# Taking a fourth token block's expert activations from gathered rows, while its value products stay dense

## The chip, the cores and the metric

The kernel runs on one core of a Trainium2 chip. The metric is device time in microseconds, the median of three runs. Each run executes the whole layer once. The profile is one further execution.

## What is computed

The reference is one layer of a streaming encoder over 1024 tokens of width 1024: a mixing part (attention over latents, "MLA", and gated linear attention, "GLA") and then an expert part, which is what the change touches. Cut to that:

```python
q = (h @ w_q).reshape(B, L, 8, 2, 128)                 # 8 heads, two halves
s = einsum('blhpd,pnd->blhpn', q, sub_keys)            # scores against 2 x 128 keys
top_s, top_i = top_k(s, 16)
...                                                    # 16 best of the 16 x 16 sums
idx  = ...                                             # expert numbers, of 128 * 128 = 16384
gate = softmax(best_s)
act  = gelu(einsum('bpd,bphkd->bphk', h, u_tab[idx]))  # one row of u for each pick
coef = act * gate
out  = einsum('bphk,bphkd->bpd', coef, v_tab[idx])     # one row of v for each pick
```

Every token picks 8 x 16 = 128 of 16384 experts. Each expert has a row of 1024 numbers in `u` and one in `v`.

## The kernel before

**Two ways through the experts.** The 1024 tokens are eight blocks of 128. Blocks 0 to 2 take the picked rows by indirect DMA ("gathers"): for each of the 128 picks one DMA brings one row of `u` for every token of the block (a tile of 128 x 1024 numbers, 512 KB) and another brings the rows of `v`. VectorE makes a dot product of each `u` tile with the tokens (L1303), ScalarE the GELU of 16 of them at a time (L1305), and VectorE adds each `v` tile, scaled, to an accumulator (L1312). That is 3 x 128 x 2 = 768 gathers. Blocks 3 to 7 (640 tokens, `ND`) go through all experts on TensorE: for each of 128 keys `e`, a u stage multiplies the tokens with 128 rows of `u` and takes the GELU; a coefficient step multiplies the result by a matrix of gates that is zero where an expert was not picked (L1433); and v stages multiply the coefficients with `v` and add up. Each product is three matmuls of a high and a low half (L80 to L82), and the low half of each 512 KB weight tile is made by VectorE (L74) once ScalarE has made the high half (L73).

**Sizes.** A u stage has 640 tokens, more than one PSUM tile holds, so it runs twice over 320 columns (`HD`): 2 x 8 x 3 = 48 matmuls for a key. A v stage works on a group `q` of four keys and one half of the output columns: 4 keys x 5 blocks x 3 = 60 matmuls of 512 columns, five PSUM tiles added to the accumulator in SBUF at L1450. A group has two such halves.

**Order of the work.** Tokens go in two groups of four blocks. After MLA, GLA and routing of group 0 follow MLA(1), mix(1) (GLA and output projection), route(1), then "build" (`gate_matrix` writes the gates of the dense blocks to HBM, d_gate), then the dense stage. The u stages of keys 0 to 21 stand in route(1), those of 22 to 53 in build (both write their activations to HBM, d_act), and those of 54 to 127 between the v stages. So the v stages of the first twelve groups have no u stage beside them, and from the end of group 11 on four u stages go with each group, the last two behind group 29.

**Pace of the gathers.** The gathers are a generator, `self.G`. `bg` steps it by `rate` gathers for each weight tile that is asked for (`weights`), and in MLA for each step of `merge`. A gather is issued by GpSimd after ScalarE's last cast (`pace`), and its VectorE work is placed behind the last low half made (`lag`). The row tiles are a ring of `NROW`; the dot or add of a row is placed NROW - 2 gathers after its issue. The rates are `R_MLA` in MLA(1) (until its last unit), `R_MIX`, `R_ROUTE`, `R_BUILD` and `R_DENSE`. By the code the calls that step the generator are 144 in MLA(1), 50 weight tiles in mix(1), 38 in route(1), 32 in the u stages of build (of which 27 by the rate of build), and 202 in the dense stage.

**Queues.** Weight tiles, gates (1280 KB for a group, 512 bytes at a stretch) and activations come by SyncE's queue, in order; gathers, and MLA's stored keys and values, by GpSimd's. A weight tile has two raw buffers (`wr`) and two pairs of halves (`wh`, `wl`).

Of the kernel before, what the change touches and what calls it, by code (L numbers as in the profile page):

```python
# [20 lines left out]
P = 128  # L21
# [11 lines left out]
NK = 128  # L33
LEVELS = (64, 32, 16, 8, 4, 2, 1)
NGB = 3
NROW = 6
DB = list(range(GB, NB)) + list(range(NGB, GB))
ND = len(DB) * P
HD = ND // 2
EG = 4  # L40
NLEAD = 54
PACE, LAG = True, True
# [9 lines left out]
BANKS = [dict(zip(("S", "tr", "mm", "pv"), map(int, str(x)))) for x in (BA, BB)]  # L52
NGA, NGR, F_MLA = 14, 14, 0.9
RA0, NRU, NLATE = 7, 22, 5
R_MLA, R_MIX, R_ROUTE, R_BUILD, R_DENSE = 0.0, 1.5, 0.6, 2.6, 3.0


class Layer:
# [85 lines left out]
    def build(self, debug=None):  # L144
# [4 lines left out]
        self.rate = 0.0  # L149
        self.owed = self.nwl = self.wlp = 0.0  # L150
        self.pref = {}
        self.raws = {}
        self.picks = {}
        with ExitStack() as ctx:
# [24 lines left out]
            self.d_gab = dt("d_gab", [2, 2 * NC, P, GT])  # L179
            self.d_h = dt("d_h", [T, D])  # L180
            self.d_n2 = dt("d_n2", [T, D])
            self.d_act = dt("d_act", [NLEAD, P, ND])
            self.d_n2t = dt("d_n2t", [2, P, NC, ND - GT]) if ND > GT else None
            self.d_gate = dt("d_gate", [P, ND // 32, NK * 32])
            self.small = self.pool(ctx, "small", 3)
            self.sm = self.small
            with ExitStack() as c0:
# [10 lines left out]
                with ExitStack() as c:  # L198
# [6 lines left out]
                    keys = self.gate_keys()[NGF:NGR]  # L205
                    self.route(0, {hp: keys[hp - RA0:hp - RA0 + 1] if hp < 15 else keys[max(15 - RA0, 0):] for hp in range(RA0, 16)}, self.lead_gate)
                    self.tokens_last()
            self.G = self.gather_all(list(range(NGB)))
            self.rate = R_MLA
            with ExitStack() as c:  # L210
                self.mh = self.pool(c, "mh", 2)
# [958 lines left out]
    def norm_ffn(self, g):  # L1170
        nc, a = self.nc, self.a
        t0 = g * GT
        hb = self.hb
        nh, nl = self.n2 = [self.t(self.arp, [P, NC, ND if g else GT], F32R, "ar", 2) for _ in range(2)]
        if g and ND > GT:
            for i, x in enumerate(self.n2):
                nc.gpsimd.dma_start(x[:, :, GT:], self.d_n2t[i].bitcast(F32R))
        gain = self.t(self.wp, [P, D], F32, "wr")
        self.bcast_row(gain, a["norm_ffn"], D)
        for b in range(GB):  # L1180
            rows = slice(t0 + b * P, t0 + (b + 1) * P)
            nc.sync.dma_start(self.d_h[rows], hb[:, b])
            n = self.row_norm(self.wk, self.sm, hb[:, b], gain)
            if g * GB + b < NGB or self.debug:
                nc.sync.dma_start(self.d_n2[rows], n)
        if g == 0 and NGF:
            self.lead_gate(self.gate_keys()[0], ("w_q", 0))
        for b in range(GB):
            self.transpose_split(self.psum, hb[:, b], nh[:, :, b * P:(b + 1) * P], nl[:, :, b * P:(b + 1) * P])
            yield  # L1190
# [15 lines left out]
    def route(self, g, fill, step):  # L1206

        nc, a = self.nc, self.a
        nh, nl = self.n2
        pk = []  # L1210
        pool = self.gp if g == 0 else self.pb
        for b in range(GB):
            d = dict(gate=self.t(pool, [P, 8, 16], F32, "gate", GB))
            if g * GB + b < NGB:
                d["idi"] = self.t(self.wk, [P, 8, 16], I32, "idi", NGB)
            else:
                d["ij"] = self.t(pool, [P, 2, 8, 16], F32, "ij", GB if g else GB - NGB)
            pk.append(d)
            self.picks[g * GB + b] = d
        rt = self.t(self.g1, [P, 4096], F32, "yl")  # L1220
        self.r_oh = [rt[:, 512 * i:512 * i + 512].rearrange("p (w i j) -> p w i j", w=2, j=16) for i in range(3)]
        self.r_sc = rt[:, 1536:2560].rearrange("p (n k) -> p n k", k=NK), rt[:, 2560:3008].rearrange("p (n k) -> p n k", k=112)
        rs = self.t(self.g1, [P, 4096], F32, "yh")
        w5 = lambda x, n: x.rearrange("p (a b c d) -> p a b c d", a=n, b=GB, c=2)
        self.r_cand = rs[:, 0:448].rearrange("p (b k) -> p b k", b=GB)
        self.r_tv = w5(rs[:, 448:576], 1)[:, 0]
        self.r_tf = w5(rs[:, 576:832], 2)
        self.r_ab = w5(rs[:, 832:1088], 2).bitcast(U32)
# [12 lines left out]
        for h in range(8):  # L1241
            s = self.t(self.wk, [P, GB, 2, NK], F32, "gt", 2)
            for p in range(2):
                hp = 2 * h + p
                extra = fill.get(hp, [])
                after = ("w_q", hp + 1) if hp < 15 else None
                nxt = (extra + [after])[0]
                pq, _, _ = self.colproj(("w_q", hp), nh, nl, GT, nxt, 2 if hp < QP else 1)
                qs = r_qs[p]
                nc.scalar.copy(qs, pq)  # L1250
                if p == 1:
                    keyscores(s, 0)
# [12 lines left out]

    def tokens_last(self):

        nc = self.nc
        if ND > GT:
            for i, x in enumerate(self.n2):  # L1270
                nc.sync.dma_start(self.d_n2t[i], x[:, :, NGB * P:].bitcast(F32))
        for b in range(NGB):
            pk = self.picks[b]
            ids = self.t(self.gp, [P, 8, 16], I32, "ids", NGB)
            nc.vector.tensor_copy(ids, pk["idi"])
            pk["idi"] = ids

    def gather_all(self, blks):

        nc = self.nc
        units = [(b, h) for b in blks for h in range(8)]
        queue, held = [], {}
        lag = lambda i: self.after(i, self.dve_last) if LAG else None

# [4 lines left out]
        def start(b):  # L1291
            n2 = self.t(self.gp, [P, D], F32, "n2b", 1)
            nc.sync.dma_start(n2, self.d_n2[b * P:(b + 1) * P])
            acc = self.t(self.gp, [P, D], F32, "acc", 1)
            nc.sync.dma_start(acc, self.d_h[b * P:(b + 1) * P])
            held[b] = n2, acc

        def dot(b, c, u):
# [4 lines left out]
            lag(nc.vector.tensor_tensor_reduce(out=u, in0=u, in1=held[b][0], op0=ALU.mult, op1=ALU.add, scale=1.0, scalar=0.0, accum_out=act[:, 0, k:k + 1]))  # L1303
            if k == 15:
                nc.scalar.activation(act[:, 1], act[:, 0], AF.Gelu)  # L1305

        def add(b, c, v):
            h, k = c // 16, c % 16
# [77 lines left out]
    def u_stage(self, e, nxt, at, behind=None):  # L1386

        n2h, n2l = self.n2
        wh, wl = self.weights(("uT", e), nxt)
        for k in range(2):  # L1390
            ts = slice(k * HD, (k + 1) * HD)
            ps = self.t(self.psum, [P, 512], F32, "tr")
            for c in range(NC):
                s = slice(c * P, (c + 1) * P)
                first = self.mm3(ps[:, :HD], wh[:, s], wl[:, s], n2h[:, c, ts], n2l[:, c, ts], c == 0, c == NC - 1)
                if c == 0 and behind is not None:
                    self.after(first, behind)
            self.nc.scalar.activation(at[:, ts], ps[:, :HD], AF.Gelu)  # L1398

    def lead_gate(self, key, nxt):  # L1400
        self.run(self.raw_gate(1, self.gate_keys().index(key), nxt, "tr", 2))
# [1 line left out]
    def lead_u(self, key, nxt):  # L1403
        e = key[1]
        if e % 6 == 0:
            self.leads = self.t(self.g1, [P, 6, ND], F32, "nl" if e % 12 else "nh", 1)
        at = self.leads[:, e % 6]
        self.u_stage(e, nxt, at)
        self.nc.sync.dma_start(self.d_act[e], at)
# [1 line left out]
    def dense(self, ctx):  # L1411
# [12 lines left out]
        def load_act(e):  # L1424
            if e < NLEAD:
                acts[e] = self.t(self.wk, [P, ND], F32, "at", NAT)
                nc.sync.dma_start(acts[e], self.d_act[e])

        def coef(q, j):
            cf = coefs[q, j] = self.t(self.wk, [P, 2, ND], F32R, "cf", NCF)  # L1430
            at = acts.pop(q * EG + j)
            at3 = at.rearrange("p (b t) -> p b t", t=32)
            (nc.gpsimd if j < CFP else nc.vector).tensor_tensor(at3, at3, gbuf[:, q % 2, :, j], ALU.mult)  # L1433
            self.split(cf[:, 0], cf[:, 1], at)

        def v_stage(q, half):
# [30 lines left out]
        def lead():  # L1467
            for x in seq[:nlead]:
                at = self.t(self.wk, [P, ND], F32, "at", NAT)
                self.u_stage(x[1], order.get(("uT", x[1])), at, self.gm_last if x[1] >= NLEAD - NLATE else None)  # L1470
                nc.sync.dma_start(self.d_act[x[1]], at)
                done[0] += 1
                yield

# [40 lines left out]
    def gate_matrix(self):  # L1515
# [3 lines left out]
        nc = self.nc  # L1519
        G8 = 8  # L1520
        iota = self.iota[:, None, :].broadcast_to([P, G8, NK])
        for d, blk in sorted(enumerate(DB), key=lambda x: x[1]):
            pk = self.picks[blk]
            stage = self.t(self.wk, [P, NK, 32], F32, "big")
            pt = self.t(self.psum, [P, 4, P], F32, "tr")
            for i in range(2):
# [97 lines left out]
```

## Time and profile before

| | us |
|---|---|
| median of three runs | 3879.04 (3875.96 to 3888.12) |
| the profiled execution, its own time | 3874.64 |
| its span, first to last instruction | 3872.9 |
| TensorE busy | 3616.7 (93%) |
| VectorE busy | 3015.7 (78%) |
| ScalarE busy | 1293.6 (33%) |
| GpSimd busy | 1572.3 (41%) |

Engines are PE (TensorE), PEld (its weight loads), DVE (VectorE), ACT (ScalarE), POOL (GpSimd) and SP (SyncE). Records of consecutive instructions of an engine overlap, so the pace of an engine is the distance from one start to the next, and a PE that is shown busy is not at its peak for that.

### The profile page before, as it was taken

The numbers are of one execution on the slowest core, as the hardware profiler recorded it, in microseconds if no ns is written. First come the engines' busy times: TensorE is split into PE (matmuls) and PEld (weight loads), VectorE is DVE, ScalarE is ACT, GpSimd is POOL, SyncE is SP. The second block draws the span as 40 slices with busy tenths as digits, with TensorE's granted clock in tenths as the row PEclk, the third lists the DMA queues.
The fourth block names the chain that finished last, engine by engine and source line by source line (L and its number), as shares of the span: only waits on it lengthen the run. The fifth ranks groups of instructions, "written<-read, shape, count | busy, mean of one in ns | idle before, by whom it ended". The sixth has DMA issues, their size and how long they took to land.

```text
span 3872.9 us, 55720 instructions
## 1 busy us (share of the span) xinstructions
PE 3616.7 (93%) x20279; PEld 3170.8 (82%) x20279; DVE 3015.7 (78%) x6477; ACT 1293.6 (33%) x2711; POOL 1572.3 (41%) x1151
## 2 busy tenths in 40 slices
PE   8899998998799899999999978999999999999999
PEld 8787797777588788788899967767888888898897
DVE  5544444389877577679999997998998888888786
ACT  4655333232366333232243432222222222222221
POOL 2432333335532232322232223444555555656562
PEclk9898998999899998999999989999999999999999
DMA  4433423442323763654467779999998988998895
GB/s 161 142 108 130 131 69 103 135 142 90 126 71 97 235 221 127 253 171 149 131 249 291 277 277 372 357 342 337 319 340 320 325 306 310 327 324 310 293 317 189
DMA packets 356628, 868.92 MB, mean 224 GB/s; under 512 B 30768, under 2 KB 150064, under 8 KB 353536
## 3 DMA queue, kind: packets, MB, share of 16 engines
q1 hardware_dynamic: 216832, 432.49, 32.1%
q0 software_dynamic: 139520, 432.87, 32.1%
q8 instruction: 159, 2.61, 0.3%
q14 instruction: 117, 0.96, 0.1%
HBM read 754.90 MB, written 110.35 MB: 223 GB/s over the span
## 4 chain that ended last, share of the span: by engine, by line
PE 41%; DVE 16%; DMA 9%; issue 3%; ACT 1%; POOL 1%; SPq 0%; DVEq 0%; ACTq 0%; POOLq 0%
PE mm L81 7%; PE mm L80 7%; PE mm L82 7%; DMA wr<-in_vb 5%; PE tr L80 5%; PE tr L82 5%; PE tr L81 5%; DVE wl L74 2%; DVE cf L1540 2%; DVE acc L1312 2%; DVE row L1303 2%; PE mm L1546 2%; DVE cf L1541 1%; DVE big L1450 1%; DMA row<-in_u,ids 1%
## 5 line engine op out<-in xcount | busy, mean ns | idle before, releaser
L73 ACT CAST wh<-wr 128x1024 fp32r<-128x1024 f32 x416 | 436.0, 1049 | 1208.0 <-PE mm L82 400.4
L100 POOL DMA_INDIRECT row<-in_v,ids x384 | 535.7, 1395 | 699.1 <-ACT wh L73 325.1
L100 POOL DMA_INDIRECT row<-in_u,ids x384 | 521.0, 1357 | 665.4 <-ACT wh L73 338.2
L80 PE MATMUL tr<-ar,wh 128*128 128x320 f32 x2048 | 638.7, 312 | 7.3 <-ACT at L1398 5.3
L82 PE MATMUL tr<-ar,wl 128*128 128x320 f32 x2048 | 633.5, 312 | 7.6 <-DVE wl L74 7.5
L81 PE MATMUL tr<-ar,wh 128*128 128x320 f32 x2048 | 636.3, 311 | 0.0
L74 DVE TENSOR_TENSOR wl<-wr,wh 128x1024 fp32r<-128x1024 f32 x322 | 395.0, 1227 | 227.3 <-ACT wh L73 220.7
L81 PE MATMUL mm<-wl,cf 128*128 128x512 f32 x1280 | 514.8, 402 | 11.4 <-DVE wl L74 11.4
L82 PE MATMUL mm<-wh,cf 128*128 128x512 f32 x1280 | 508.3, 397 | 0.0
L1312 DVE SCALAR_TENSOR_TENSOR acc<-row,act,acc 128x1024 f32<-128x1024 f32 x384 | 491.2, 1279 | 4.1 <-DMA row<-in_v,ids 3.5
L80 PE MATMUL mm<-wh,cf 128*128 128x512 f32 x1280 | 451.3, 403 | 35.4 <-ACT wh L73 28.7
L1303 DVE CUSTOM_DVE_ANT_0 row<-row,n2b 128x1024 f32<-128x1024 f32 x384 | 469.2, 1226 | 16.1 <-DMA row<-in_u,ids 16.0
L80 PEld LDWEIGHTS tr<-ar,wh 128*128 128x128 f32 x2048 | 388.7, 190 | 11.9 <-ACT at L1398 5.5
L82 PEld LDWEIGHTS tr<-ar,wl 128*128 128x128 f32 x2048 | 387.0, 190 | 10.3 <-DVE wl L74 10.1
L81 PEld LDWEIGHTS tr<-ar,wh 128*128 128x128 f32 x2048 | 388.4, 190 | 3.5
L74 POOL TENSOR_TENSOR wl<-wr,wh 128x1024 fp32r<-128x1024 f32 x94 | 230.3, 2453 | 333.8 <-ACT wh L73 323.9
L80 PEld LDWEIGHTS mm<-wh,cf 128*128 128x128 f32 x1280 | 241.3, 190 | 105.5 <-ACT wh L73 34.1
L81 PEld LDWEIGHTS mm<-wl,cf 128*128 128x128 f32 x1280 | 243.1, 190 | 76.0 <-DVE wl L74 20.2
L82 PEld LDWEIGHTS mm<-wh,cf 128*128 128x128 f32 x1280 | 243.2, 190 | 55.9
L1450 DVE TENSOR_TENSOR big<-mm,big 128x512 f32<-128x512 f32 x320 | 204.5, 679 | 20.6 <-PE mm L82 20.3
L1546 PE MATMUL mm<-cf,cf 128*128 128x128 f32 x1280 | 162.6, 284 | 27.8 <-DVE cf L1541 27.1
L1546 PEld LDWEIGHTS mm<-cf,cf 128*128 128x128 f32 x1280 | 157.2, 199 | 30.2 <-issue 22.4
(430 smaller groups left out, 7500.4 us busy)
## 6 DMA issues: line engine op xcount, KB each, us to landing
wr<-in_uT SPq DMA_DIRECT2D x128, 512.0 KB
wr<-in_vb SPq DMA_DIRECT2D x128, 512.0 KB
d_gate<-big SPq DMA_DIRECT2D x20, 2048.0 KB
big<-d_gate SPq DMA_DIRECT2D x32, 1280.0 KB
at<-d_act SPq DMA_DIRECT2D x54, 320.0 KB
wr<-in_w_q SPq DMA_DIRECT2D x32, 512.0 KB
d_act<-at SPq DMA_DIRECT2D x32, 320.0 KB
wr<-in_w_ga SPq DMA_DIRECT2D x16, 512.0 KB
```

The lines of the kernel that those rows point to most:

```text
L73: self.pace = self.nc.scalar.copy(hi, src)
L74: i = (eng or self.nc.vector).tensor_tensor(lo, src, hi.bitcast(F32), ALU.subtract)
L80: first = mm(ps, lh, rh, start=start, stop=False)
L81: mm(ps, lh, rl, start=False, stop=False)
L82: self.pe_last = mm(ps, ll, rh, start=False, stop=stop)
L100: i = self.nc.gpsimd.indirect_dma_start(out=out, out_offset=None, in_=self.a[table], in_offset=bass.IndirectOffsetOnAxis(ap=idx, axis=0))
L1303: lag(nc.vector.tensor_tensor_reduce(out=u, in0=u, in1=held[b][0], op0=ALU.mult, op1=ALU.add, scale=1.0, scalar=0.0, accum_out=act[:, 0, k ...
L1312: lag(nc.vector.scalar_tensor_tensor(acc, v, act[:, 1, k:k + 1], acc, ALU.mult, ALU.add))
L1450: nc.vector.tensor_tensor(o, ps[b], o, ALU.add)
L1540: nc.vector.tensor_scalar(gh[:, k], self.iota, tt[:, 1, t + k:t + k + 1], tt[:, 2, t + k:t + k + 1], ALU.is_equal, ALU.mult)
L1541: nc.vector.tensor_tensor(oh, iota, tb(0), ALU.is_equal)
L1546: self.gm_last = nc.tensor.matmul(ps[:, k], oh[:, kk], gh[:, kk], start=True, stop=True)
```

## The change

Blocks 0 to 2 stay as they are, and so do the v stages of blocks 3 to 7. Block 3 gets its 128 x 128 activations from gathered rows of `u`, as blocks 0 to 2 do; they are multiplied into its gates, and the products go through `gate_matrix` in place of the gates, so that its part of the coefficient needs no further product: ScalarE copies it (128 columns) and VectorE's product shrinks to 512 columns. The u stage is left with blocks 4 to 7, 512 tokens, in one pass of 24 matmuls. Block 3's gathers (128 of `u`, none of `v`) stand first in the order; `gate_matrix` takes block 3 last and would first step the gathers as far as its coefficients need. The stored transposes of block 3 (d_n2t) fall away, its normed rows are kept in d_n2, stored activations shrink from 320 to 256 KB for a key, the ring of rows has seven tiles, and three rates rise.

```diff
-NROW = 6
+NROW = 7
 DB = list(range(GB, NB)) + list(range(NGB, GB))
 ND = len(DB) * P
-HD = ND // 2
+NU = GB * P
...
-R_MLA, R_MIX, R_ROUTE, R_BUILD, R_DENSE = 0.0, 1.5, 0.6, 2.6, 3.0
+R_MLA, R_MIX, R_ROUTE, R_BUILD, R_DENSE = 0.3, 2.6, 0.6, 3.0, 3.0
...
-            self.G = self.gather_all(list(range(NGB)))
+            self.G = self.gather_all(list(range(NGB, GB)), list(range(NGB)))
...
-        nh, nl = self.n2 = [self.t(self.arp, [P, NC, ND if g else GT], F32R, "ar", 2) for _ in range(2)]
-        if g and ND > GT:
-            for i, x in enumerate(self.n2):
-                nc.gpsimd.dma_start(x[:, :, GT:], self.d_n2t[i].bitcast(F32R))
+        nh, nl = self.n2 = [self.t(self.arp, [P, NC, GT], F32R, "ar", 2) for _ in range(2)]
...
-            if g * GB + b < NGB or self.debug:
+            if g * GB + b < GB or self.debug:
                 nc.sync.dma_start(self.d_n2[rows], n)
...
-    def gather_all(self, blks):
+    def gather_all(self, half, blks):
...
-        units = [(b, h) for b in blks for h in range(8)]
+        units = [(b, h) for b in half + blks for h in range(8)]
...
-            acc = self.t(self.gp, [P, D], F32, "acc", 1)
-            nc.sync.dma_start(acc, self.d_h[b * P:(b + 1) * P])
+            acc = None
+            if b in blks:
+                acc = self.t(self.gp, [P, D], F32, "acc", 1)
+                nc.sync.dma_start(acc, self.d_h[b * P:(b + 1) * P])
...
                 nc.scalar.activation(act[:, 1], act[:, 0], AF.Gelu)
+                if b in half:
+                    gate = self.picks[b]["gate"][:, h]
+                    nc.vector.tensor_tensor(gate, act[:, 1], gate, ALU.mult)
+                    if h == 7:
+                        self.coefs_of.add(b)
...
+                    if what is add and b in half:
+                        continue
...
-        for k in range(2):
-            ts = slice(k * HD, (k + 1) * HD)
-            ps = self.t(self.psum, [P, 512], F32, "tr")
-            for c in range(NC):
-                s = slice(c * P, (c + 1) * P)
-                first = self.mm3(ps[:, :HD], wh[:, s], wl[:, s], n2h[:, c, ts], n2l[:, c, ts], c == 0, c == NC - 1)
...
-            self.nc.scalar.activation(at[:, ts], ps[:, :HD], AF.Gelu)
+        ps = self.t(self.psum, [P, 512], F32, "tr")
+        for c in range(NC):
+            s = slice(c * P, (c + 1) * P)
+            first = self.mm3(ps, wh[:, s], wl[:, s], n2h[:, c], n2l[:, c], c == 0, c == NC - 1)
...
+        self.nc.scalar.activation(at[:, 0:NU], ps, AF.Gelu)
...
-            (nc.gpsimd if j < CFP else nc.vector).tensor_tensor(at3, at3, gbuf[:, q % 2, :, j], ALU.mult)
+            m = NU // 32
+            nc.scalar.copy(at3[:, m:], gbuf[:, q % 2, m:, j])
+            nc.vector.tensor_tensor(at3[:, :m], at3[:, :m], gbuf[:, q % 2, :m, j], ALU.mult)
             self.split(cf[:, 0], cf[:, 1], at)
...
-        for d, blk in sorted(enumerate(DB), key=lambda x: x[1]):
+        for d, blk in enumerate(DB):
             pk = self.picks[blk]
+            while blk < GB and blk not in self.coefs_of:
+                next(self.G)
```

## Rows read from the trace of the kernel before

**Rows 1.** Busy time by stage: window, length, each engine, granted clock, DMA share, GB/s.
```profile
1023.00:1276.00 253.00, 233.53 (x1450) 198.14 (x1448) 183.68 (x546) 153.27 (x547) 82.53 (x97) 0.96 0.32 89
1276.00:1660.00 384.00, 361.57 (x1992) 311.05 (x1992) 258.76 (x403) 130.22 (x225) 117.53 (x95) 0.95 0.63 217
1660.00:1953.00 293.00, 273.71 (x1632) 253.25 (x1632) 268.59 (x1087) 88.10 (x139) 81.02 (x52) 0.97 0.46 147
1953.00:2353.00 400.00, 369.54 (x2754) 366.66 (x2752) 382.66 (x870) 147.21 (x257) 106.82 (x80) 0.97 0.78 285
2407.00:2758.00 351.00, 328.99 (x1340) 253.19 (x1339) 332.98 (x439) 78.27 (x94) 171.45 (x129) 0.97 0.94 343
2758.00:3798.00 1040.00, 1019.32 (x5605) 915.59 (x5604) 900.68 (x1137) 257.49 (x374) 612.56 (x437) 0.99 0.89 317
```

**Rows 2.** PSUM additions of the v stages (L1450) in the last two stages.
```profile
2407.00:2758.00 351.00, 71.27 (x111) 0.97 0.94 343
2758.00:3798.00 1040.00, 112.91 (x181) 0.99 0.89 317
```

**Rows 3.** PE in order of time, u then v matmuls: start, length, instruction.
```profile
3204.07 0.31 PE L80 MATMUL tr<-ar,wh 128*128 128x320 f32 x1
...
3205.68 0.31 PE L82 MATMUL tr<-ar,wl 128*128 128x320 f32 x1
...
3208.17 0.39 PE L80 MATMUL mm<-wh,cf 128*128 128x512 f32 x1
...
3211.44 0.39 PE L82 MATMUL mm<-wh,cf 128*128 128x512 f32 x1
```

**Rows 4.** DVE in order of time in the dense stage.
```profile
3769.62 1.21 DVE L74 TENSOR_TENSOR wl<-wr,wh 128x1024 fp32r<-128x1024 f32 x1
3770.75 1.27 DVE L1312 SCALAR_TENSOR_TENSOR acc<-row,act,acc 128x1024 f32<-128x1024 f32 x1
3771.95 1.21 DVE L1303 CUSTOM_DVE_ANT_0 row<-row,n2b 128x1024 f32<-128x1024 f32 x1
...
3773.09 1.27 DVE L1312 SCALAR_TENSOR_TENSOR acc<-row,act,acc 128x1024 f32<-128x1024 f32 x1
```

**Rows 5.** The coefficient product: busy us, mean ns of one, idle before it.
```profile
L1433 DVE TENSOR_TENSOR at<-at,big 128x640 f32<-128x640 f32 x128 | 103.8, 815 | 11.9 <-DMA big<-d_gate 8.6 <-issue 1.4 <-DMA at<-d_act 1.3
```

**Rows 6.** The stretch of 100 us with the highest DMA rate, all engines.
```profile
2500.00:2600.00 100.00, 94.06 (x389) 72.02 (x387) 95.32 (x126) 22.16 (x26) 45.33 (x36) 1.00 0.97 361
```

**Rows 7.** Waits in 2353 to 2700 and in 2700 to 3787: total us, times, longest.
```profile
ACT wh L73 <- DMA wr<-in_vb: 74.0, 19, 7.7
...
ACT wh L73 <- DMA wr<-in_vb: 105.6, 19, 9.5
```

**Rows 8.** PE in order of time behind one such late load.
```profile
3199.50 1.84 PE L80 MATMUL mm<-wh,cf 128*128 128x512 f32 x5 [2.39 <-ACT wh L73]
3201.14 0.47 PE L80 MATMUL tr<-ar,wh 128*128 128x320 f32 x1
3201.40 0.47 PE L81 MATMUL tr<-ar,wh 128*128 128x320 f32 x1
```

**Rows 9.** Gathers issued (L100, POOL) in mix(1), build and the second dense stage.
```profile
1276.00:1660.00 384.00, 105.34 (x74) 0.95 0.63 217
...
1953.00:2353.00 400.00, 106.82 (x80) 0.97 0.78 285
...
2758.00:3798.00 1040.00, 612.56 (x437) 0.99 0.89 317
```

**Rows 10.** GLA and output projection of group 0 (no gathers) and of group 1.
```profile
397.00:781.00 384.00, 356.31 (x2053) 305.56 (x2054) 169.09 (x247) 127.37 (x237) 133.98 (x72) 0.95 0.36 111
1283.00:1661.00 378.00, 361.64 (x1992) 310.93 (x1992) 259.76 (x405) 131.22 (x227) 115.85 (x92) 0.95 0.61 215
```

**Rows 11.** DVE at the end: the last gathered row, the last PSUM additions.
```profile
3828.06 1.27 DVE L1312 SCALAR_TENSOR_TENSOR acc<-row,act,acc 128x1024 f32<-128x1024 f32 x1
...
3863.22 3.49 DVE L1450 TENSOR_TENSOR big<-mm,big 128x512 f32<-128x512 f32 x5 [8.89 <-PE mm L82]
```

More of the change, by code (lines that the diff above doesn't have):

```diff
@@ L151, in build @@
         self.pref = {}
+        self.coefs_of = set()
         self.raws = {}
@@ L181, in build @@
             self.d_n2 = dt("d_n2", [T, D])
-            self.d_act = dt("d_act", [NLEAD, P, ND])
-            self.d_n2t = dt("d_n2t", [2, P, NC, ND - GT]) if ND > GT else None
+            self.d_act = dt("d_act", [NLEAD, P, NU])
             self.d_gate = dt("d_gate", [P, ND // 32, NK * 32])
@@ L1213, in route @@
             d = dict(gate=self.t(pool, [P, 8, 16], F32, "gate", GB))
-            if g * GB + b < NGB:
-                d["idi"] = self.t(self.wk, [P, 8, 16], I32, "idi", NGB)
-            else:
+            if g == 0:
+                d["idi"] = self.t(self.wk, [P, 8, 16], I32, "idi", GB)
+            if g * GB + b >= NGB:
                 d["ij"] = self.t(pool, [P, 2, 8, 16], F32, "ij", GB if g else GB - NGB)
@@ L1268, in tokens_last @@
         nc = self.nc
[L1269 to L1272, printed above, removed]
+        for b in range(GB):
             pk = self.picks[b]
-            ids = self.t(self.gp, [P, 8, 16], I32, "ids", NGB)
+            ids = self.t(self.gp, [P, 8, 16], I32, "ids", GB)
             nc.vector.tensor_copy(ids, pk["idi"])
             pk["idi"] = ids
-    def gather_all(self, blks):
+    def gather_all(self, half, blks):
         nc = self.nc
-        units = [(b, h) for b in blks for h in range(8)]
+        units = [(b, h) for b in half + blks for h in range(8)]
         queue, held = [], {}
@@ L1389, in u_stage @@
         wh, wl = self.weights(("uT", e), nxt)
-        for k in range(2):
-            ts = slice(k * HD, (k + 1) * HD)
-            ps = self.t(self.psum, [P, 512], F32, "tr")
-            for c in range(NC):
-                s = slice(c * P, (c + 1) * P)
-                first = self.mm3(ps[:, :HD], wh[:, s], wl[:, s], n2h[:, c, ts], n2l[:, c, ts], c == 0, c == NC - 1)
-                if c == 0 and behind is not None:
-                    self.after(first, behind)
-            self.nc.scalar.activation(at[:, ts], ps[:, :HD], AF.Gelu)
+        ps = self.t(self.psum, [P, 512], F32, "tr")
+        for c in range(NC):
+            s = slice(c * P, (c + 1) * P)
+            first = self.mm3(ps, wh[:, s], wl[:, s], n2h[:, c], n2l[:, c], c == 0, c == NC - 1)
+            if c == 0 and behind is not None:
+                self.after(first, behind)
+        self.nc.scalar.activation(at[:, 0:NU], ps, AF.Gelu)
     def lead_gate(self, key, nxt):
@@ L1405, in lead_u @@
         if e % 6 == 0:
-            self.leads = self.t(self.g1, [P, 6, ND], F32, "nl" if e % 12 else "nh", 1)
+            self.leads = self.t(self.g1, [P, 6, NU], F32, "nl" if e % 12 else "nh", 1)
         at = self.leads[:, e % 6]
@@ L1426, in load_act @@
                 acts[e] = self.t(self.wk, [P, ND], F32, "at", NAT)
-                nc.sync.dma_start(acts[e], self.d_act[e])
+                nc.sync.dma_start(acts[e][:, 0:NU], self.d_act[e])
         def coef(q, j):
@@ L1470, in lead @@
                 self.u_stage(x[1], order.get(("uT", x[1])), at, self.gm_last if x[1] >= NLEAD - NLATE else None)
-                nc.sync.dma_start(self.d_act[x[1]], at)
+                nc.sync.dma_start(self.d_act[x[1]], at[:, 0:NU])
                 done[0] += 1
```

## The prediction

> **What bounds the kernel now.** I read the busy times by stage first, then the last two stages one group of keys at a time, then who waits for whom in them, and last the stages in which the added gathers are to go. The reader should see that no single engine bounds the whole kernel [rows 1]. In MLA(1) and mix(1) PE is busy for 92 to 94% and DVE for 73% and 67%. In route(1) both are above 90%, in build DVE has 383 of 400 us. Then come two dense stages. The first has v stages alone: 110 PSUM additions, ten for a group, so 11 groups in 351 us or 31.9 us each [rows 2]; there DVE is busy 95% of the time and DMA runs at 343 GB/s [rows 1]. The second has 180 additions, 18 groups, in 1040 us, 57.8 us each [rows 2], with PE at 98%, DVE at 87% and DMA at 317 GB/s [rows 1].
>
> PE's pace there is read from starts. Eleven steps between u matmuls of 320 columns take 1.61 us, 0.146 each; fourteen steps between v matmuls of 512 columns take 3.27 us, 0.234 each [rows 3]. A group of the second dense stage has 120 v matmuls (28.0 us) and 4 x 48 u matmuls (28.1 us): 56.1 of the 57.8 us. PE is the bound there, with 1.7 us lost.
>
> **The change, part by part.**
>
> *The u stage.* 48 steps of 0.146 (7.03 us) become 24 of 0.234 (5.61 us): 1.42 us less PE for each of 128 keys, 182 us in all. It counts only where PE is the bound.
>
> *The second dense stage.* With the u part at 22.4 us PE needs 50.5 us a group; with the 1.7 us that it loses now, 52.2. But the gathers keep their rate of 3.0, and the others are close. DVE is busy 901 us for 18 groups, 50.0 each [rows 1]; the coefficient product goes from 640 to 512 columns, and by length 815 ns [rows 5] become about 650, four times 0.16 less: 49.4 us. At the share that DVE reached in the first dense stage (333 of 351) that is 52.0 us. DMA moves 57.8 us x 317 GB/s = 18.3 MB a group, and nothing of it goes away, since activations of these keys are not stored. At the first stage's mean of 343 GB/s [rows 1] it takes 53.4 us; at the best 100 us of the trace, 361 GB/s [rows 6], 50.7. Three resources within 1.5 us of each other do not all run at their best, so I take the slowest, 53.4: 4.4 us a group, **-79 us** for 18. From below the bound is PE's 52.2 (-101). From above it is the late load described under the rivals, 56.3 (-27).
>
> The Trainium skill's page "DMA: Bandwidth & Descriptors", section Specifications, gives about 358 GB/s as what one core gets from HBM. By that figure the 18.3 MB take an estimated 51.1 us, PE's 52.2 would bind and the term would be -101; this trace holds such a rate for 100 us but not as the mean of a stage.
>
> ScalarE's added copy of 128 columns lies beside an engine busy 257 of 1040 us [rows 1], and its GELU becomes one instruction instead of two: nothing. It stands in front of the casts in ScalarE's queue, so a late gate load would now hold it there rather than on DVE; the weights' casts would wait too.
>
> *The first dense stage.* It has no u stages, so only the coefficient product (0.65 us a group) and the stored activations (4 x 64 KB, 0.26 MB, 0.8 us at 343 GB/s) shrink: 0.6 us for 12 groups, **-7** (0 to -9).
>
> *The added gathers, 128 of u.* A dot takes 1.14 us of DVE from start to start, an add 1.20, a weight's low half 1.13 [rows 4]. Their places follow from rates times calls. MLA(1): 0.3 x 144 = 43 where there were none. Mix(1): 2.6 x 50 = 130 instead of 75 (74 recorded [rows 9]). Build: 27 x 0.4 = 11 more than 80 [rows 9]. Route as before. Dense: 3.0 x 202 = 606, so that the 896 end with the last weight tile.
>
> In MLA(1) the 43 dots are 49 us of DVE; it has 69 us idle of 253 [rows 1] and would come to 92%. The softmax chain passes through DVE, and what queues behind a dot is the next maximum or low half, for which PE's value products wait. Bounds 0 to 49 us. The nearest row is GLA: the group without gathers takes 384 us with 169 us of DVE, the group with 75 gathers and the weights' low halves on DVE takes 378 us with 260 us [rows 10], so 91 us more DVE cost nothing. MLA ends nearer to saturation, so I take **+15**.
>
> In mix(1) 55 more gathers, nearly all dots, are 62 us of DVE: 260 + 62 of 378, 85%. A wait is added too: block 0's first gather asks for its tokens in a tile that block 3's last dots, five gathers later, still read, and SP's queue of weight tiles stands behind that load for about two tiles. It stands so already between blocks. Bounds 0 to 62; by rows 10, **+10**.
>
> Build is DVE's [rows 1]: 11 x 1.17 = **+13** (0 to 13), and its u stages' 45 us of PE lie hidden behind DVE. After build PE's last u stages wait less, but the gates' way through HBM follows: **-2** (0 to -8).
>
> Route(1): 22 u stages give PE 31 us, but DVE is busy 269 of 293 us [rows 1] and its work is unchanged: -4 (0 to -24). In the first routing eight small DVE instructions come in: +1. Together **-3**.
>
> *The end.* The last gathered row is now added at 3829 us, 34 us before the last PSUM additions [rows 11]. With gathers up to the last tile the last two groups run at the first dense stage's 31.9 us instead of PE's 28.0: about +4 and +2, and the last adds +3; two u stages behind group 29 give 3 back: **+6** (0 to 12).
>
> *The ring of seven rows* gives each gather one more step to land: nothing, or a small gain.
>
> Sum: -79 - 7 + 15 + 10 + 13 - 2 - 3 + 6 = -47. Against the profiled 3874.6 us that is 3828; the median of the runs lies 4.4 us above it, so **3832 us**.
>
> **The rivals.**
>
> *A. PE stays the bound.* DMA holds the rate of rows 6 for the whole stage and DVE hides its dots. For: rows 10; against: 317 and 343 GB/s as means [rows 1]. Then -101 in the second dense stage, +3 for MLA, 0 for mix and +11 in build, with -15 for the rest: -102, about 3777. The Trainium skill's figure of about 358 GB/s ("DMA: Bandwidth & Descriptors", Specifications) would lead here as well.
>
> *B. The late load takes the gain.* In each group one tile of `v` queues behind the gates: 19 waits of 5.6 us on average in the second stage [rows 7], about one a group. Mostly PE just covers it; once it idled 2.39 us and then stepped at 0.265 us instead of 0.146 [rows 8], at a lower granted clock. The tile is asked for two stages ahead, and two u stages that are 1.42 us shorter each take away up to 2.9 us of cover. If all of it shows, with ten steps at 0.265 (1.2 us), a group takes 52.2 + 2.9 + 1.2 = 56.3 us: 27 instead of 79, sum +5, 3884. Against it: most groups run with no idle on PE.
>
> *C. Slower: the gathers of MLA(1) and mix(1) are paid in full.* Both stages have in-order chains through DVE. 49 + 62 = 111 instead of 25 us: +39, 3918. It turns the sign once 72 of the 111 us, two thirds, are exposed. For it: 92% in MLA(1); against it: rows 10.
>
> *D. The change does not do what it says:* `gate_matrix` has to wait for block 3's coefficients. They need 133 gathers; 43 + 130 + 23 = 196 are issued before build. Practically excluded.
>
> **How the numbers follow.** Forecast (3800 to 3865) 0.51, A (3765 to 3800) 0.16, B 0.14, C 0.17, D 0.02. About 0.3% (12 us) is what a measurement of this kernel can tell from no change. Faster: forecast, A and a third of B, 0.72. Same: half of B and the mild end of C, 0.09. Slower: the rest, 0.19. The range leaves out the better half of A and the worse part of C: 3785 to 3895; the forecast's own is 3800 to 3865.
>
> **What would show it.** 1024 u matmuls a line of 512 columns at 0.234 us; the second dense stage at 52 to 55 us a group, with DVE and DMA near 95% and PE below 97%; 43 gathers in MLA(1), that stage 5 to 30 us longer; build 13 us longer; the last add within 10 us of the last PSUM additions. The forecast is wrong if the groups stay above 56 us or MLA(1) and mix(1) together grow by over 70.

## The result: slower by 1.7%

After: 3941.37 us, median of four runs (3930.74 to 3952.29). Before, on the same chip: 3877.50 (3874.16 to 3888.12, four runs). Ratio 1.0168, 95% interval 1.0146 to 1.0191. The forecast was 3832, with a range of 3785 to 3895. The profiled execution took 3949.66 us, 75.0 more than that of before.

Busy time by stage in the changed kernel, the same stages as [rows 1] (window, length, PE, PEld, DVE, ACT, POOL, granted clock, DMA share, GB/s):

```profile
1027.00:1313.00 286.00, 246.21 (x1436) 206.22 (x1437) 230.23 (x639) 158.93 (x550) 134.55 (x150) 0.91 0.54 160
1313.00:1733.00 420.00, 374.18 (x2010) 320.16 (x2009) 323.05 (x537) 143.74 (x240) 208.50 (x147) 0.92 0.77 267
1733.00:2027.00 294.00, 254.48 (x1135) 203.44 (x1134) 275.67 (x1099) 88.29 (x123) 80.38 (x56) 0.94 0.47 153
2027.00:2427.00 400.00, 336.48 (x2008) 294.46 (x2007) 393.56 (x887) 138.35 (x225) 111.88 (x90) 0.96 0.77 284
2478.00:2825.00 347.00, 324.01 (x1334) 253.59 (x1335) 330.42 (x442) 89.92 (x138) 171.28 (x131) 0.98 0.95 342
2825.00:3871.00 1046.00, 953.46 (x3878) 746.71 (x3877) 889.65 (x1137) 250.24 (x373) 581.40 (x436) 0.96 0.88 314
```

Route(1), build and the first dense stage are as they were within 5 us. MLA(1) grew by 33 us and mix(1) by 36 in these windows, and the second dense stage, which was to shrink by 79, is 6 longer although PE's work in it fell by 66 us (1019 to 953). DMA there runs slower than before, at 314 GB/s against 317: it is not the bound.

PSUM additions (L1454) in the two dense stages, which count the groups as in [rows 2]:

```profile
2478.00:2825.00 347.00, 70.73 (x109) 0.98 0.95 342
2825.00:3871.00 1046.00, 114.95 (x180) 0.96 0.88 314
```

The 180 additions are 18 groups in 1046 us: 58.1 a group, against 57.8. The gathers issued in MLA(1) and in mix(1) are about those that the rates gave (43 and 130):

```profile
1027.00:1313.00 286.00, 47.16 (x45) 0.91 0.54 160
1313.00:1733.00 420.00, 196.60 (x127) 0.92 0.77 267
```

**Where the second dense stage waits.** The longest waits on DMA and on a cast in it (total us, times, longest):

```profile
ACT wh L73 <- DMA wr<-in_uT: 190.0, 13, 17.3
...
PE tr L80 <- ACT wh L73: 55.6, 13, 6.9
```

In [rows 7] it was a tile of `v` that came late, 19 times, 5.6 us each. Now it is a tile of `u`, 13 times, 14.6 us each, and 13 times PE stands 4.3 us. One of these 13, in order of time: SP's issues, ScalarE's casts, then PE (start, length, instruction, idle before it):

```profile
3012.25 0.52 SPq L1424 DMA_DIRECT2D big<-d_gate  x1
3013.38 7.60 SPq L873 DMA_DIRECT2D wr<-in_uT  x1
...
3015.35 1.05 ACT L73 CAST wh<-wr 128x1024 fp32r<-128x1024 f32 x1 [5.27 <-PE mm L82]
3031.54 1.04 ACT L73 CAST wh<-wr 128x1024 fp32r<-128x1024 f32 x1 [15.13 <-DMA wr<-in_uT]
...
3032.64 0.80 PE L80 MATMUL tr<-ar,wh 128*128 128x512 f32 x1 [4.72 <-ACT wh L73]
...
3034.92 0.63 PE L81 MATMUL tr<-ar,wh 128*128 128x512 f32 x1
3035.34 0.63 PE L82 MATMUL tr<-ar,wl 128*128 128x512 f32 x1
...
3037.20 0.39 PE L81 MATMUL tr<-ar,wh 128*128 128x512 f32 x1
3037.43 0.39 PE L82 MATMUL tr<-ar,wl 128*128 128x512 f32 x1
```

The tile is asked for 1.1 us behind the gates and is cast 18.2 us later. PE idles 4.72 us and then steps at 0.43 us for a while, where 0.23 is its pace; the granted clock in 3031 to 3036 is 0.50, the 1.2 GHz level. Of the 18 groups those with a `u` tile behind the gates took 57.4 to 62.3 us, three with a tile of `v` there that was cast within 15 us took 53.1 to 54.5; a fourth tile of `v`, cast 19.1 us after it was asked for, went with a group of 60.1.

**The page.** The chain of work that ended last, by line, has the loads of `u` tiles as its largest entry; and of the u stage's matmuls (now 1024 a line, of 512 columns) those that need a high or a low half waited 60.2 and 56.0 us, where the kernel before had 7.3 and 7.6:

```profile
DMA wr<-in_uT 6%; PE mm L80 5%; PE mm L81 5%; PE mm L82 5%; DVE row L1300 5%; DVE wl L74 4%; DVE acc L1314 4%; DVE cf L1546 3%; DVE big L1454 3%; DVE cf L1547 2%; DMA wr<-in_vb 2%; PE tr L82 2%; PE tr L80 2%; PE tr L81 1%; DMA row<-in_u,ids 1%
...
L80 PE MATMUL tr<-ar,wh 128*128 128x512 f32 x1024 | 424.2, 414 | 60.2 <-ACT wh L73 58.9
L82 PE MATMUL tr<-ar,wl 128*128 128x512 f32 x1024 | 426.5, 417 | 56.0 <-DVE wl L74 55.6
```

### The profile page after: what moved, and what is told of

Same layout as the page of the kernel before. It is cut to its first block, busy times and chain, and to the rows that moved or that the text cites. A ratio compares the mean times of both kernels' runs of the same rounds, so it can differ in the third digit from the quotient of the medians.

```text
span 3947.9 us, 50029 instructions
## 1 busy us (share of the span) xinstructions
PE 3516.2 (89%) x17207; PEld 2889.3 (73%) x17207; DVE 3142.0 (80%) x6750; ACT 1310.3 (33%) x2733; POOL 1710.0 (43%) x1277
## 4 chain that ended last, share of the span: by engine, by line
DVE 35%; PE 26%; DMA 12%; issue 6%; ACT 3%; POOL 1%; SPq 0%; DVEq 0%; ACTq 0%; POOLq 0%
DMA wr<-in_uT 6%; PE mm L80 5%; PE mm L81 5%; PE mm L82 5%; DVE row L1300 5%; DVE wl L74 4%; DVE acc L1314 4%; DVE cf L1546 3%; DVE big L1454 3%; DVE cf L1547 2%; DMA wr<-in_vb 2%; PE tr L82 2%; PE tr L80 2%; PE tr L81 1%; DMA row<-in_u,ids 1%
## 5 line engine op out<-in xcount | busy, mean ns | idle before, releaser
L100 POOL DMA_INDIRECT row<-in_u,ids x512 | 715.8, 1398 | 878.8 <-ACT wh L73 374.6
L100 POOL DMA_INDIRECT row<-in_v,ids x384 | 482.3, 1256 | 566.1 <-ACT wh L73 249.7
L1300 DVE CUSTOM_DVE_ANT_0 row<-row,n2b 128x1024 f32<-128x1024 f32 x512 | 622.1, 1227 | 17.1 <-DMA row<-in_u,ids 17.0
L80 PE MATMUL tr<-ar,wh 128*128 128x512 f32 x1024 | 424.2, 414 | 60.2 <-ACT wh L73 58.9
L82 PE MATMUL tr<-ar,wl 128*128 128x512 f32 x1024 | 426.5, 417 | 56.0 <-DVE wl L74 55.6
L81 PE MATMUL tr<-ar,wh 128*128 128x512 f32 x1024 | 419.5, 410 | 0.0
L82 PEld LDWEIGHTS tr<-ar,wl 128*128 128x128 f32 x1024 | 201.8, 197 | 127.3 <-DVE wl L74 79.9
L80 PEld LDWEIGHTS tr<-ar,wh 128*128 128x128 f32 x1024 | 202.9, 198 | 111.3 <-ACT wh L73 64.9
L81 PEld LDWEIGHTS tr<-ar,wh 128*128 128x128 f32 x1024 | 201.8, 197 | 47.7
L1454 DVE TENSOR_TENSOR big<-mm,big 128x512 f32<-128x512 f32 x320 | 205.6, 681 | 29.5 <-PE mm L82 29.2
```

The source lines that it names most:

```text
L80: first = mm(ps, lh, rh, start=start, stop=False)
L81: mm(ps, lh, rl, start=False, stop=False)
L82: self.pe_last = mm(ps, ll, rh, start=False, stop=stop)
L100: i = self.nc.gpsimd.indirect_dma_start(out=out, out_offset=None, in_=self.a[table], in_offset=bass.IndirectOffsetOnAxis(ap=idx, axis=0))
L1454: nc.vector.tensor_tensor(o, ps[b], o, ALU.add)
```

## The experiments

Lengths of stages in us, from the traces: MLA(1) from the last index of routing to the last value product, mix(1) to the last addition into `h`, the dense stages between last PSUM additions of groups 0, 11 and 29 (the second one for a group). The runs follow below.

| kernel | us | ratio to before | MLA(1) | mix(1) | build | first dense | second, a group |
|---|---|---|---|---|---|---|---|
| before | 3877.5 | | 255.0 | 386.7 | 375.5 | 351.1 | 57.8 |
| after | 3941.4 | 1.0168 | 286.7 | 420.4 | 374.7 | 346.5 | 58.1 |
| e1_u_alone | 3808.3 | 0.9792 (0.9739 to 0.9845) | 253.0 | 382.5 | 368.5 | 348.8 | 55.5 |
| e2_short_dots | 3892.4, one run | | 262.5 | 393.6 | 380.7 | 357.8 | 57.2 |
| e3_no_gather | 3936.8, one run | | 284.9 | 417.1 | 374.6 | 350.5 | 57.8 |
| e4_gate_rows | 3852.2 | 0.9901 (0.9872 to 0.9931) | 289.7 | 415.9 | 379.3 | 341.5 | 53.2 |
| e5_before_gate_rows | 3843.6 | 0.9897 (0.9879 to 0.9914) | 254.2 | 387.5 | 376.3 | 344.4 | 56.1 |
| e6_gate_queue | 3856.6 | 0.9935 (0.9915 to 0.9956) | 284.1 | 419.2 | 374.9 | 344.9 | 52.6 |
| e7_rates | 3863.3 | 0.9947 (0.9926 to 0.9968) | 253.9 | 413.7 | 386.1 | 353.0 | 55.3 |
| e8_low_half_pool | 3875.5 | 0.9976 (0.9962 to 0.9989) | 284.2 | 441.1 | 399.7 | 343.9 | 52.2 |
| e9_pool_and_rates | 3875.0 | 0.9978 (0.9964 to 0.9991) | 256.1 | 476.4 | 382.8 | 339.9 | 52.5 |

**1. The shorter u stage alone** (after, without the gathers, dots and coefficients of block 3, rates of before):

```diff
-R_MLA, R_MIX, R_ROUTE, R_BUILD, R_DENSE = 0.3, 2.6, 0.6, 3.0, 3.0
+R_MLA, R_MIX, R_ROUTE, R_BUILD, R_DENSE = 0.0, 1.5, 0.6, 2.6, 3.0
...
-        self.coefs_of = set()
+        self.coefs_of = set(range(NGB, GB))
...
-            self.G = self.gather_all(list(range(NGB, GB)), list(range(NGB)))
+            self.G = self.gather_all([], list(range(NGB)))
```

> The changed kernel with the shorter u stage alone: block 3's 128 gathers and dots are left out (its coefficient is then the bare gate, so its part of the output is not the layer's), and the rates are those of before, so MLA(1) and mix(1) have 0 and 75 gathers again. Theory L (one weight tile behind the gate load in SyncE's queue is late in each group, whatever stands in the early stages): MLA(1) and mix(1) go back to about 255 and 387 us from 287 and 420, and the second dense stage stays at 57 to 60 us a group instead of the 53.4 forecast; total about 3870, no gain over before. Theory V (the early gathers also slow the dense stage, through order or state that they leave behind): groups fall to 52 to 54 us, total about 3790.

Measured: 3808.31 us. MLA(1) and mix(1) are those of before again, so their growth belongs to the added gathers and dots. The second dense stage stands between the two expectations, at 55.5 us a group: even without block 3's gathers ScalarE waits 106.8 us for tiles of `u` and 92.5 us for tiles of `v`, so the late tile takes part of the gain there by itself. The other part, 2.6 us a group less than with the gathers, is not explained by this run.

**2 and 3. Which part of a gather costs?** In the second run block 3's dots are a copy of one column, with all gathers issued. In the third the dots run at full length on the token tile, and block 3's gathers are not issued.

```diff
 # e2_short_dots
-            lag(nc.vector.tensor_tensor_reduce(out=u, in0=u, in1=held[b][0], ...
+            if b in half:
+                lag(nc.vector.tensor_copy(act[:, 0, k:k + 1], u[:, 0:1]))
+            else:
+                lag(nc.vector.tensor_tensor_reduce(out=u, in0=u, in1=held[b][0], ...
 # e3_no_gather
-            lag(nc.vector.tensor_tensor_reduce(out=u, in0=u, ...
+            lag(nc.vector.tensor_tensor_reduce(out=u, in0=held[b][0] if b in half else u, ...
...
-                    self.gather(row, table, ...
+                    if b not in half:
+                        self.gather(row, table, ...
```

> The changed kernel with all its gathers, but the 128 dots of block 3 (1.14 us of VectorE each) are replaced by a copy of one column (under 0.2 us), so block 3's activations are wrong numbers. Theory D (VectorE's slots in front of the chains of MLA and GLA are what the 32 and 34 us of MLA(1) and mix(1) are made of): MLA(1) falls from 287 to 258 to 264 us, mix(1) from 420 to 390 to 396. Theory G (issuing on GpSimd and the transfers make it, with the dots a side matter): both stay within 8 us of 287 and 420. The dense stages stay as they are by both.

> The other half of the same test: the 128 dots of block 3 run, on the token tile itself, but its 128 gathers are not issued, so GpSimd and the DMA engines are spared and block 3's activations are wrong numbers. Theory D (VectorE's slots): MLA(1) stays at 280 to 287 us and mix(1) at 412 to 420. Theory G (gathers): they fall to 255 to 265 and 387 to 397. If both this and the run with short dots fall half way, both causes add.

MLA(1) and mix(1) in the one and in the other, columns as above:

```profile
1025.00:1287.00 262.00, 235.80 (x1446) 199.59 (x1447) 189.79 (x598) 159.06 (x551) 128.76 (x147) 0.94 0.56 174
1287.00:1680.00 393.00, 362.62 (x2004) 309.87 (x2002) 230.59 (x451) 141.91 (x239) 180.33 (x148) 0.94 0.80 286
```

```profile
1022.00:1308.00 286.00, 245.26 (x1448) 205.96 (x1448) 231.88 (x641) 159.55 (x551) 89.05 (x106) 0.92 0.35 96
1308.00:1724.00 416.00, 371.27 (x2002) 317.72 (x2001) 322.42 (x538) 141.38 (x238) 78.28 (x63) 0.93 0.43 153
```

Without the gathers (DMA down from 160 to 96 GB/s in MLA(1)) both stages stay as long as in the change, within 4 us. Without the dots' VectorE time MLA(1) gives back 24 of its 32 us and mix(1) 27 of 34. These are theory D's numbers in both runs. Each is one run; the change itself and runs 4, 6 and 8, which have all 43 gathers and dots in MLA(1), took 284 to 290 us there. What the added gathers cost is in the main VectorE's slots: the growth is about 0.7 us for each of the 43 dots added in MLA(1) and 0.6 for each of the 55 in mix(1), of which the short dots give back 0.56 and 0.49. The rest is not told apart: each short dot still holds a copy of 0.14 us. VectorE was not saturated (230 of 286 and 323 of 420 us). PE is late in two ways. From the first matmul of MLA(1) to its last value product it stands 36 us, where it stood 18 in the kernel before, and it steps slower: in the windows, 1436 matmuls take 246.2 us at a granted 0.91, where 1450 took 233.5 at 0.96 [rows 1].

**4. Gates in long rows.** The gates of a group are stored in one stretch of 10 KB a partition, where the change (and the kernel before) has 20 stretches of 512 bytes.

```diff
-self.d_gate = dt("d_gate", [P, ND // 32, NK * 32])
+self.d_gate = dt("d_gate", [P, NK // EG, ND // 32, EG * 32])
-nc.sync.dma_start(gt..., self.d_gate[:, :, q * EG * 32:(q + 1) * EG * 32])
+nc.sync.dma_start(gt..., self.d_gate[:, q].rearrange("p b x -> p (b x)"))
-nc.sync.dma_start(self.d_gate[:, d * 4 + t32], stage.rearrange("p j t -> p (j t)"))
+nc.sync.dma_start(self.d_gate[:, :, d * 4 + t32], stage.rearrange("p (g e) t -> p g (e t)", e=EG))
```

> The changed kernel with the gates stored by group of four keys, so that one partition's gates of a group are 10 KB in a row instead of 20 pieces of 512 bytes; the pieces are now in the write of build. Nothing else changes. Theory L (the weight tile behind the gate load is late because 2560 small packets share the DMA engines one by one with the gathers' packets of 4 KB): the load behind the gates lands 5 us or more sooner, PE's wait for it goes, the second dense stage falls from 58.1 to 52 to 55 us a group, 60 to 100 us in all; build may grow by up to 10. Theory S (the stage is saturated by VectorE's 49 us and DMA's 18 MB a group, or the two raw weight buffers are too few): it stays above 56.5 us a group, total within 30 us of 3941.

Measured: 53.2 us a group, 3852.15 us, as theory L expected. The second dense stage, and the same place in it as above (SP, then ScalarE):

```profile
2827.00:3785.00 958.00, 922.88 (x3882) 732.31 (x3881) 889.22 (x1137) 252.53 (x373) 582.39 (x436) 0.99 0.92 344
```

```profile
3012.19 0.33 SPq L1424 DMA_DIRECT2D big<-d_gate  x1
3013.32 0.33 SPq L873 DMA_DIRECT2D wr<-in_uT  x1
...
3024.26 1.05 ACT L73 CAST wh<-wr 128x1024 fp32r<-128x1024 f32 x1 [7.10 <-DMA wr<-in_uT]
```

The same two loads are issued at the same times, and the tile is cast 10.9 us later instead of 18.2. What the DMA engines did from 3013 to 3031 us in the change, and in this run (packets and rate, then q0, the gathers' queue, and q1, SP's):

```profile
DMA packets 3969, 6.39 MB, mean 355 GB/s; under 512 B 174, under 2 KB 2734, under 8 KB 3967
q0 software_dynamic: 1113, 4.03, 56.9%
q1 hardware_dynamic: 2854, 2.33, 39.3%
```

```profile
DMA packets 1744, 7.16 MB, mean 398 GB/s; under 512 B 192, under 2 KB 192, under 8 KB 1614
q0 software_dynamic: 1296, 4.72, 65.8%
q1 hardware_dynamic: 446, 2.41, 33.9%
```

And the change again, in the 4 us from 3022 to 3026 alone:

```profile
q0 software_dynamic: 376, 1.37, 83.9%
q1 hardware_dynamic: 440, 0.25, 20.6%
```

In the 18 us of the change SP's queue spends 2854 packets on 2.33 MB; the gates of a group are 128 x 20 = 2560 pieces of 512 bytes. The tile behind them in that queue gets through after them, while the gathers' queue moves 4.03 MB; SyncE's issue of the tile alone lasts 7.60 us, 0.33 in this run. With long rows 446 packets do for 2.41 MB. Whether order or packet size is the price needs run 6.

**5. The same layout without the change.** The three lines of run 4 in the kernel before.

> The kernel before, with the gates of a group stored in one stretch of 10 KB a partition (20 of 512 bytes before), nothing else. Question: is the layout a gain of its own, or one that only the shorter u stage can use? Theory N (needs the change): before, PE's 56.1 us a group stand against 57.8 measured, so at most 1.7 us of a group can come back: second dense stage 1010 to 1020 us (56.1 to 56.7 a group), the first as it was (351, less up to 10), 3840 to 3855 in all, ratio 0.991 to 0.994. The change then costs nothing against it: 3852 with the change and the same layout, so all that the u stage gives is used up in MLA(1) and mix(1). Rival P (the packets, not the order, are the price): long rows free more of the DMA, gathers land earlier and VectorE's ring stalls less, the first dense stage falls by over 15 us as well, below 3835. Rival Z: PE covered the late tile before, groups stay above 57.4, 3865 or more.

Its second dense stage:

```profile
2757.00:3767.00 1010.00, 1009.20 (x5603) 910.59 (x5602) 900.33 (x1137) 258.37 (x373) 613.55 (x437) 1.00 0.89 326
```

Measured: 3843.62 us, theory N: groups at 56.1 us, which is PE's pace alone (28.0 + 28.1), with PE busy in 1009 of 1010 us. The 1.7 us a group that PE lost before was the late tile: ScalarE's 105.6 us of waiting for tiles of `v` [rows 7] have no counterpart in this run. Against this kernel the change with the same layout gains nothing: the two ratios, 0.9897 and 0.9901, cannot be told apart. By their profiled spans (3841.6 and 3861.5) it takes 52 us off the second dense stage and adds 36 in MLA(1), 28 in mix(1), 9 in the first half and 8 in route(1); the profiled execution of run 4 was the longest of its seven.

**6. Order or packets?** The change with its gates in 512-byte pieces, loaded from ScalarE's queue, so that no weight tile stands behind them.

```diff
-nc.sync.dma_start(gt..., self.d_gate[:, :, ...
+nc.scalar.dma_start(gt..., self.d_gate[:, :, ...
```

> The changed kernel with its gates in 512-byte pieces as it has them, but the load issued from ScalarE's queue in place of SyncE's; all else the same. Weight tiles then no longer stand behind the gates in one queue. Theory F (order in the queue): the tile was late because it stood behind a load that trickles; now only the gates are late, and they are asked for a group ahead. Second dense stage 52.5 to 54.5 us a group, about 3855 to 3870. Rival S (the small pieces take the time from every queue): the tile shares the engines with 2560 packets of 512 bytes and the gathers wherever it stands, 57 to 58 us a group, about 3935. Between (55 to 56.5): both.

The second dense stage; then two of its groups (3100 to 3204), and PE's waits in these:

```profile
2829.00:3777.00 948.00, 919.82 (x3882) 729.53 (x3881) 887.91 (x1136) 252.57 (x373) 582.98 (x436) 0.99 0.94 347
...
3100.00:3204.00 104.00, 101.46 (x432) 80.46 (x431) 97.45 (x127) 28.32 (x42) 64.42 (x48) 1.00 0.93 347
```

```profile
PE tr L82 <- DVE wl L74: 2.5, 2, 1.3
```

The loads in the stage, with the median time from issue to landing in us at the end:

```profile
wr<-in_vb SPq DMA_DIRECT2D x72, 512.0 KB, 6.8
wr<-in_uT SPq DMA_DIRECT2D x72, 512.0 KB, 6.8
big<-d_gate ACTq DMA_DIRECT2D x17, 1280.0 KB, 28.0
```

Measured: 52.6 us a group with the small packets left in place, theory F. The gates now take 28.0 us to land and nothing waits for them, while a weight tile takes 6.8. The cost was the place in the queue: a weight tile behind a load that takes long because each of its packets is small. In a regular group (52.3 us; 11 of the 18 lie within 1 us of it) PE does 216 matmuls at 0.234, 50.5 us, and waits 1.3 us for one of VectorE's low halves.

**7. Can the rates be chosen better?** Run 4 with no gathers in MLA(1) and 3.25 a tile in the dense stage.

```diff
-R_MLA, R_MIX, R_ROUTE, R_BUILD, R_DENSE = 0.3, 2.6, 0.6, 3.0, 3.0
+R_MLA, R_MIX, R_ROUTE, R_BUILD, R_DENSE = 0.0, 2.6, 0.6, 3.0, 3.25
```

> The changed kernel with the gates in long rows, no gather in MLA(1) (rate 0 for 0.3) and 3.25 for 3.0 in the dense stage, so that the 43 gathers of MLA(1) move to the dense stage. Question: what does a dot cost there, against the 0.7 us that it costs in MLA(1)? Theory D (VectorE's slots): MLA(1) back to 253 to 257 us, about 32 less; the dense stages carry 43 more rows of 1.17 us, 50 us of VectorE; the first has no room (95% busy), the second little (93%), so they take 30 to 50 us more in all: no gain, 3845 to 3875. Rival R (the rates were the mistake): the second dense stage hides them behind its 50.5 us of PE a group, dense grows by under 15 us, and the whole comes to 3825 to 3840.

Measured: 3863.30 us, theory D. MLA(1) falls by 36 us and the two dense stages grow by 11.5 and 38: some 1.1 us for each of 43 rows there, more than the 0.7 of MLA(1). Whether VectorE sets that price is not shown: the added rows are DMA's work too, which ran at 348 GB/s in the second dense stage, the highest mean of any run. Its profiled span is that of run 4, 3861.5 us.

**8 and 9. Making room on VectorE.** Run 4 with the low halves of mix(1)'s weight tiles on GpSimd; then, in addition, MLA(1)'s gathers moved into mix(1).

```diff
                     self.rate = R_MIX
+                    self.wlp = 1.0
...
                     self.rate = R_ROUTE
+                    self.wlp = 0.0
 # e9_pool_and_rates only
-R_MLA, R_MIX, R_ROUTE, R_BUILD, R_DENSE = 0.3, 2.6, 0.6, 3.0, 3.0
+R_MLA, R_MIX, R_ROUTE, R_BUILD, R_DENSE = 0.0, 3.4, 0.6, 3.0, 3.0
```

> The changed kernel with the gates in long rows, and the low halves of mix(1)'s weight tiles (47 of 1.22 us on VectorE) made by GpSimd, as group 0 has them (2.5 us there); rates as in the change. If VectorE's slots are what the dots of mix(1) cost (theory D), the stage goes from 416 us back to 385 to 395, VectorE to about 265 us busy, and the whole to 3820 to 3835, under the 3844 of the kernel before with the same gate layout. Rival G (GpSimd's queue is the next wait): a low half takes 2.5 us there and stands behind gathers of 1.1 to 1.5 us, so PE waits for GpSimd instead: mix(1) 405 us or more, 3840 to 3860.

> As the run with mix(1)'s low halves on GpSimd, and the 43 gathers of MLA(1) moved into mix(1) (rates 0.0 and 3.4 for 0.3 and 2.6), so that the dense stage keeps its number. Theory D: MLA(1) back to 254 us (35 less), mix(1) with 170 dots at the load on VectorE that 128 had with the low halves there: 395 to 415 us; 3800 to 3825 in all. Rival G: 170 gathers and 47 low halves are about 350 us of GpSimd in a stage of 400, low halves late, mix(1) over 425, 3830 or more.

Both missed theory D's times: mix(1) took 441 and 476 us. Its dots in the first of them (busy, mean ns, idle before), then the largest wait there:

```profile
L1302 DVE CUSTOM_DVE_ANT_0 row<-row,n2b 128x1024 f32<-128x1024 f32 x118 | 179.2, 1539 | 45.9 <-DMA row<-in_u,ids 45.8
```

```profile
POOL wl L74 <- ACT wh L73: 82.8, 22, 16.4
...
PE mm L81 <- POOL wl L74: 10.1, 5, 4.8
PE mm L82 <- POOL wl L74: 9.3, 7, 2.6
```

Rival G's mechanism is part of it: PE waited 19.4 us for GpSimd's low halves, where in run 4 it waited 3.7 for VectorE's, and 41.4 us in run 9. Two things came on top that G did not name, and run 8 lies above G's range too. GpSimd, with its queue in order, stands up to 16.4 us on a low half whose cast has not come, and the gathers behind it are issued late: VectorE then waits 45.8 us for rows. And a dot takes 1539 ns on average in place of the 1219 of the change, 38 us for 118 of them. VectorE was not freed, then: it was busy 348 of 440 us without the low halves, 324 of 416 with them in run 4. So moving the low halves is no way to free VectorE here, and these runs say nothing against theory D, which rests on runs 2 and 3.

## Why the prediction was wrong

The ledger of the profiled executions, forecast and measured, in us:

| step | forecast | measured |
|---|---|---|
| first half, up to the last index of routing (forecast within routes) | +1 | +10 |
| MLA(1) | +15 | +32 |
| mix(1) | +10 | +34 |
| route(1) | -4 | +4 |
| build | +13 | -1 |
| build to group 0 | -2 | -5 |
| first dense stage | -7 | -5 |
| second dense stage | -79 | +7 |
| last two groups and end | +6 | -1 |
| sum | -47 | +75 |

**The failed step: "At the first stage's mean of 343 GB/s ... it takes 53.4 us ... 4.4 us a group", the term of -79 us.** It is 86 of the 122 us missed. The step took DMA's rate for what bounds a group. In the changed kernel a group took 58.1 us at 314 GB/s, for in 13 of 18 PE stood on the tile behind the gates and then stepped slowly. The rows named that tile already [rows 7, 8]; the step left it out and put it under rival B. The amount is about what the stage takes once the late tile is gone, 53.2 us at 344 GB/s in run 4 and 52.6 at 347 in run 6, but that is partly luck: a regular group of run 6 is PE's 50.5 us and 1.3 us of waiting for VectorE, not DMA's bytes at a mean rate.

**Rival B had the mechanism, and a bound that was no bound.** It forecast 56.3 us a group from the cover that PE loses (2.9 us) and ten slow steps (1.2), with the tile as late as before. The tile became later, 14.6 us of idle ScalarE instead of 5.6, and in 13 groups it was a tile of `u`. The 55.6 us of idle PE and, if all 13 groups are like the one shown, nine steps of 0.2 us too much in each (23 us) are three quarters of the 104 us that separate 18 groups of 58.1 from the regular 52.3. Its slow steps were priced at 320 columns, 0.265 us for 0.146; in the changed stage they have 512 and take 0.43 for 0.23. "From above it is the late load" was reasoned with a lateness that the change itself raised. Why SP's order puts a `u` tile there in the changed program was not tried.

**Second failed step: "91 us more DVE cost nothing ... by rows 10, +10" and MLA(1)'s +15.** These two terms were mis-sized by 41 us. [Rows 10] showed that mix(1) takes 75 gathers at no cost; it was read as if the next 55 were free as well, and they cost 0.6 us each. MLA(1) has no such row at all. Rival C's place and cause were right (runs 2 and 3), its price too high: 66 of the 111 us that it put at risk were paid. With all else as forecast these 41 us would have turned -47 into -6, no change; the first failed step alone gives +39, and it needed both to end near +75.

**Right or nearly:** the u step at 0.234 us for 512 columns; the first dense stage; the number of gathers in MLA(1) and mix(1); ScalarE's copy, for which PE did not wait in the second dense stage; the last gathered add beside the last PSUM additions. Build's +13 did not come. The first half took 1021 to 1032 us in the runs that have the same instructions there as the change, so its +10 is partly scatter. In rival A's sum the -15 for the rest does not follow from the forecast's own terms, which give -6; no conclusion hangs on it.

## What to carry to other kernels

- Look at what stands in front of a critical transfer in its own queue. A load of small pieces that is itself asked for early can still cost every group, and the cure was worth 85 us (one line, run 6) or 89 us (a layout, run 4) to the changed kernel and about 40 to the one before. Without it the shorter u stage, which by the prediction's working saves PE 182 us, showed as a loss; with it in both kernels, as no gain.
- An engine that is 67 to 73% busy in a stage with chains through it is not free: here each added instruction of 1.2 us made the stage 0.6 to 0.7 us longer. That a stage took some work at no cost does not price the work that comes on top of it.
- Price a change against the kernel with the small repair, too: before with the gate layout runs in 3843.6 us, the lowest time here of a kernel that leaves no work out.

## What the hardware showed that was not expected

- **One queue is not like another.** In the change's window above, 2854 packets of SP's queue moved 2.33 MB in 39% of the engines' time, beside gathers that moved 4.03 MB in 1113 packets. From 3022 to 3026 us the two moved about as many packets, 440 and 376, and the gathers five times the bytes, 1.37 MB against 0.25 (shown at run 4). The Trainium skill's page "DMA: Bandwidth & Descriptors", section Queues, rings and completion order, says that a DMA engine takes turns between its queues packet by packet; the trace agrees, in that the queue of small packets got few bytes for its turns. The Trainium skill's same page, section Issuing engines are not separate DMA queues, says that issuing from several engines at once saves only the sequencer's time, which is usually small beside the DMA. Run 6 differs: the same load issued from ScalarE took a group from 58.1 to 52.6 us, since the tiles no longer stood behind it.
- **A dot slows beside GpSimd's low halves**, from 1219 to 1539 ns on average (run 8). Of the 118 dots, the 84 that overlap no low half of GpSimd took 1219 ns as before, and the 34 that overlap one took 2329, the longest 3875. The Trainium skill's page "SBUF — State Buffer", section Who interferes with whom, says that a VectorE instruction with two SBUF inputs and a GpSimd instruction that reads SBUF contend, and that one of them waits for the whole of the other; the trace agrees with it.
- **DMA held 398 GB/s for 18 us** in run 4, a shorter stretch than the 100 us of [rows 6], whose 361 the prediction took as the best rate; as the mean of the second dense stage no run had more than 348 (run 7). The 18 us also lie above the figure of about 358 that the prediction cites.
